# Delta rule on its two diagonal 64-token blocks: quadrant products, and the two scan directions interleaved

## The chip, the cores and the metric

One core of one Trainium2 chip runs the whole network as one program. The metric is the device time of one execution in microseconds (us); lower is better. Three runs of the kernel before took 3878.19, 3879.66 and 3897.93 us.

## The reference, cut to what matters

The reference is a stack of mixer and feed-forward blocks on 512 tokens of width 1024. Only one mixer is touched: the gated delta rule ("gdn") of the first block. It has 4 heads of key and value width 128, runs over 256 context tokens and then 512 latent tokens, once in each direction (d = 0 and d = 1), and works in chunks of 64 tokens:

```python
gc = jnp.cumsum(g, axis=-1)                                  # inside a chunk of 64
decay = jnp.exp(jnp.where(lower, gc[..., :, None] - gc[..., None, :], -jnp.inf))
lmat = jnp.where(strict, jnp.einsum('bhncd,bhnsd->bhncs', kb, k) * decay, 0.0) + jnp.eye(CHUNK)
rhs = jnp.concatenate([v * beta[..., None], kb * jnp.exp(gc)[..., None]], axis=-1)
sol = lax.linalg.triangular_solve(lmat, rhs, left_side=True, lower=True, unit_diagonal=True)
u0, kcd = sol[..., :dv], sol[..., dv:]
...
def step(s, inp):                                            # over the chunks, in order
    u = u0_i - jnp.einsum('bhcd,bhde->bhce', kcd_i, s)
    s_new = s * gl_i[..., None, None] + jnp.einsum('bhcd,bhce->bhde', kd_i, u)
    o = jnp.einsum('bhcd,bhde->bhce', qd_i, s) + jnp.einsum('bhcs,bhse->bhce', attn_i, u)
```

So each chunk needs the inverse of a unit triangular 64x64 matrix per head, some products with it, and two products per step of the recurrence.

## The kernel before, in words

Every array is fp32. The mixer treats 128 tokens (two chunks) as one **unit** (d, t): 6 tiles t of 128 tokens (t = 4, 5 are the context) in 2 directions, 12 units. The 12 units are dealt to three groups k = 0, 1, 2 of four (`gdn_front`, `self.steps`). The [128, 4, 128] tiles of a unit hold, for each of the 4 heads, a 128x128 matrix of which only the two 64x64 blocks on the diagonal are used: the two chunks. The rest is masked to zero.

A unit passes through these functions:

- `gdn_prep1` (line 881): loads a row of decays to all partitions (`gg`, line 897), forms the decay differences and their exponentials (`ga`, `gb`, on VectorE, ScalarE, GpSimd), multiplies with K K^T (TensorE, `lg<-kT`) to the matrix `gC`, and writes it to DRAM (`dC`). For latent units it also makes the masked Q K^T (`gat`) and the decayed queries (`gE`).
- `gdn_solve` (line 950), once for four units: reads the 16x16 diagonal blocks of the four `dC` back with one block per partition (`cb`), inverts them by 15 pairs of VectorE instructions (`xw`, `xb`), and writes them to `dX`.
- `gdn_prep2` (line 967): loads X (the block-diagonal inverse), transposes it to Y, and doubles the inverse twice (16 to 32 to 64) by products `lg<-gY,gC`, `lg<-gX,qz`, `lg<-qz,gX` with VectorE updates between them. Then it makes u0 and kcd (`gu`, `gkc`) by products with `gv`, and `gkd`.
- `gdn_scan` (line 1024): two steps (one for each chunk of the unit): p1 = kcd S (`sm<-gS,gkc`), uu = u0 - p1 on VectorE (`guu`), p2 = kd^T uu (`sm<-guu,gkd`), and the new state, four VectorE instructions, one for each head (`gS`). Latent units also accumulate the output (`mm<-gE,gS`, `mm<-gat,guu`), which `add_out` evicts.

`gdn_front` runs prep1 of groups 0 and 1 and both solves; at the same time the projection `ab_z` (full-size products) and the normalisation of the other mixer run. `ab_scan(k)` then runs prep2 of two units (one of each direction), their two scans, and so on; inside `ab_scan(0)` lie prep1 and the solve of group 2. The code gives a data flow: a planner orders the instructions of each engine by their priority (order in the code) and by when their inputs are ready, so groups of different units stand interleaved in each engine's queue, and each queue then runs in its order. All DMAs named here are issued from SP's queue. PSUM has banks `lg` x3, `sm` x2, `mm` x2, `lo` x1 at that time.

One fp32 product is two records in the trace, each a weight load (PEld) and a matmul (PE); the text calls such a pair a **pass**. A fp32 transpose is one.

Of the kernel before, what the change touches and what calls it, by code (L numbers as in the profile page):

```python
# [19 lines left out]
P = 128  # L20
# [11 lines left out]
class Net:  # L32
# [397 lines left out]
    def ab(self, dbg):  # L430
# [10 lines left out]
        with ExitStack() as left:  # L441
# [8 lines left out]
            lreset, masks = bp.tile([P, 256], F32, name="lreset"), bp.tile([P, 5, P], F32, name="masks")  # L450
# [343 lines left out]
    def bc4(self, ap2):  # L794

        return ap2.unsqueeze(1).to_broadcast([P, 4, P])
# [20 lines left out]
    def ab_scan(self, k, z=None):  # L817

        if k == 0:
            self.qz = []  # L820
            for l in range(2):
                for e in range(2):
                    q = self.up3.tile([P, 4, P], F32, name="qz%d%d" % (l, e))
# [45 lines left out]
    def scratch(self, zero):  # L869
        self.dC = [self.dram.tile([4, 16512], F32, name=f"dC{i}") for i in range(12)]  # L870
        self.dX = [self.dram.tile([4, 16512], F32, name=f"dX{i}") for i in range(12)]
        for t in self.dX:
            self.nc.sync.dma_start(self.whole(t), zero)

    def gtile(self, tag, bufs, pool=None):
        return (self.up2 if pool is None else pool).tile([P, 4, P], F32, name=tag, tag=tag, bufs=bufs)
# [3 lines left out]

    def gdn_prep1(self, d, t, k, i):

# [3 lines left out]
        def u(tag, bufs, pool=self.up):  # L886
            return self.gtile(tag, bufs, pool)
# [3 lines left out]
        s = slice(t * P, t * P + P)  # L891
        r0 = 32 + 32 * d
# [6 lines left out]
        self.tt(dif, self.bcl(gcc), pg, ALU.subtract)  # L899
# [4 lines left out]
        self.tt(wk[0:64], pg[0:64, :, l0], gcc[0:64], ALU.subtract)  # L904
        self.tt(wk[64:128], pg[64:128, :, l1], gcc[64:128], ALU.subtract)
# [4 lines left out]
        if lat:  # L910
            E = r["E"] = u("gE", 4, keep)
            self.act(E, pg, AF.Exp)
# [4 lines left out]
        pk = v4(self.pt("lg"))  # L917
        for h in range(4):
            self.mm(pk[:, h], kT[:, h, s], kT[:, h, s])
# [4 lines left out]
        if d == 0:  # L924
            self.tt(C, C, self.bcl(beta), ALU.mult)
        else:
            pb = u("gg", 3)
            nc.sync.dma_start(pb, self.gd[12:16, s].partition_broadcast(P))
            self.tt(C, C, pb, ALU.mult)
        nc.sync.dma_start(self.whole(self.dC[4 * k + i]), C)  # L930
        if lat:
            self.gt(r["E"], r["E"], qT[:, :, s], ALU.mult)
            pa = v4(self.pt("lg"))
            for h in range(4):
                self.mm(pa[:, h], kT[:, h, s], qT[:, h, s])
            a1 = u("gb", 2)
            self.gt(a1, Da, self.bc4(self.masks[:, 3 + d]), ALU.mult)
            at = r["at"] = u("gat", 4, keep)
            self.tt(at, a1, pa, ALU.mult)
        return r  # L940

    def whole(self, t):

        return t[:, :16384].rearrange("h (p c) -> p h c", c=P)

    def diag(self, t):

        return t.rearrange("h (b r) -> (h b) r", r=2064)[:, :2048].rearrange("b (i c) -> b i c", c=P)[:, :, 0:16]
# [18 lines left out]
    def gdn_prep2(self, d, t, k, i, r):  # L967

        nc, v4, u = self.nc, self.v4, self.gtile
# [3 lines left out]
        X = u("gX", 3, self.up3)  # L973
        nc.sync.dma_start(X, self.whole(self.dX[4 * k + i]))
        C = r.pop("C")
        pt = v4(self.pt("lg"))
        for h in range(4):
            self.tr(pt[:, h], X[:, h])
        Y = u("gY", 3, self.up3)
        nc.scalar.copy(Y, pt)  # L980
        for l in range(2):
# [3 lines left out]
            half = lambda ps: ps[:, :256].rearrange("p (h m c) -> p h m c", h=4, c=b)  # L985
            pq = half(self.pt("lg"))
            for h in range(4):
                self.mm(pq[:, h], C[:, h], part(Y, 1)[:, h])
            Q = self.qz[2 * l + self.nq % 2]
            self.tt(part(Q, 1), pq, part(self.bc4(self.masks[:, 1 + l]), 1), ALU.mult)  # L990
            if l == 0 or d == 1:
                px = half(self.pt("lg"))
                for h in range(4):
                    self.mm(px[:, h], Q[:, h], part(X, 0)[:, h])
            if l == 0 or d == 0:
                py = half(self.pt("lg"))
                for h in range(4):
                    self.mm(py[:, h], X[:, h], part(Q, 1)[:, h])
# [15 lines left out]
        for h in range(4):  # L1014
            self.mm(pu[:, h], W[:, h], vb[:, h])
        u0 = r["u0"] = u("gu0", 3)
        nc.scalar.copy(u0, pu)
        pc = v4(self.pt("lg"))
        for h in range(4):
            self.mm(pc[:, h], kb[:, h], W[:, h])  # L1020
        kc = r["kc"] = u("gkc", 3)
        nc.scalar.copy(kc, pc)

    def gdn_scan(self, d, t, r):
        nc, v4, u = self.nc, self.v4, self.gtile
        lat = t < 4
        s = slice(t * P, t * P + P)
        S = self.S[d]
        u0, kc, kd, gl = r["u0"], r["kc"], r["kd"], r["gl"]
        uu = u("guu", 2)  # L1030
        po = v4(self.pt("mm")) if lat else None
        first = True
        for j in ((0, 1) if d == 0 else (1, 0)):
            p = slice(64 * j, 64 * j + 64)
            if S is None:
                nc.vector.tensor_copy(uu[p], u0[p])
            else:
                p1 = v4(self.pt("sm"))
                for h in range(4):
                    self.mm(p1[p, h], kc[:, h, p], S[:, h])  # L1040
                self.tt(uu[p], u0[p], p1[p], ALU.subtract)
            p2 = v4(self.pt("sm"))
            for h in range(4):
                self.mm(p2[:, h], kd[p, h], uu[p, h])
            if lat:
# [917 lines left out]
```

## Time and profile before

| | |
|---|---|
| median of three runs | 3879.66 us |
| profiled execution, whole | 3887.8 us |
| its span, first to last instruction | 3885.6 us |
| TensorE busy / VectorE busy / ScalarE busy | 97% / 54% / 34% |
| stage A (prep1, solves, `ab_z`): 397 to 465 us | 68 us |
| stage B (prep2, scans): 465 to 690 us | 225 us |

The two stages are cut where the trace shows the first and the last of their instructions: the transposes of the first X start at 465 us, the last products of the last scan end near 692 us. Everything after belongs to the layers that the change doesn't touch. PE is TensorE's matmuls, PEld its weight loads, DVE is VectorE, ACT ScalarE, POOL GpSimd, SP the queue of the DMAs. PEclk is the granted TensorE clock as a share of 2.4 GHz; its two levels here are 1.0 and 0.5 (1.2 GHz). A tile written `64*128` in a row is rows x columns of the array that an instruction uses.

### The profile page before, as it was taken

Reading aid. Unit: us, or ns where it says so; the run is one execution under the profiler, and the core shown is the slowest. Engines: PE = TensorE matmul, PEld = TensorE weight load, DVE = VectorE, ACT = ScalarE, POOL = GpSimd, SP = SyncE. Lnnn points to the kernel's source line nnn. Section 1 sums busy time; section 2 is a strip of 40 time slices with the busy share of each in tenths; the row PEclk is TensorE's granted clock in tenths of the full one; section 3 lists DMA queues with packets and bytes.
Section 4 is the critical chain, followed back from the end, with each engine's and each line's share of the span. In section 5 each row is a group of like instructions: output and inputs, shape, how many; then the busy total and the mean of one; then the engine's idle time right before and its main releaser. Section 6 shows DMA issues by size and latency. Waiting matters only on the chain.

```text
span 3885.6 us, 45987 instructions
## 1 busy us (share of the span) xinstructions
PE 3763.5 (97%) x18062; PEld 3045.1 (78%) x18062; DVE 2095.3 (54%) x3391; ACT 1331.0 (34%) x2082; POOL 173.3 (4%) x200
## 2 busy tenths in 40 slices
PE   6999899999999999999999999999999999999998
PEld 3887688788878878887888748888788876788886
DVE  7656875655458863335434585434643445554345
ACT  6445511322333333224222453222432333332223
POOL 1000310000003300000000000000000000000000
PEclk9999789999999999999999999999999998999999
DMA  6411542366433233322332303333333231223332
GB/s 202 150 55 45 132 120 61 103 185 208 122 117 92 80 112 110 96 91 90 98 98 92 79 12 92 98 93 97 97 98 98 92 93 35 64 82 97 98 98 76
DMA packets 386902, 384.78 MB, mean 99 GB/s; under 512 B 40939, under 2 KB 349355, under 8 KB 386688
## 3 DMA queue, kind: packets, MB, share of 16 engines
q1 hardware_dynamic: 385720, 381.57, 32.1%
q8 instruction: 142, 2.33, 0.3%
q14 instruction: 72, 0.59, 0.0%
q10 hardware_dynamic: 968, 0.29, 0.0%
HBM read 363.47 MB, written 18.27 MB: 98 GB/s over the span
## 4 chain that ended last, share of the span: by engine, by line
PE 90%; DVE 6%; ACT 2%; issue 1%; DMA 1%; POOL 0%; DVEq 0%; SPq 0%; ACTq 0%; POOLq 0%
PE mm L145 24%; PE mm L146 24%; PE mm L147 24%; PE lg L150 3%; PE sm L150 3%; PE mm L150 3%; PE po L150 2%; PE sm L154 1%; DVE sqa L106 1%; PE po L145 1%; PE lo L150 1%; PE po L147 1%; PE po L146 1%; PE lg L145 1%; PE lg L146 0%
## 5 line engine op out<-in xcount | busy, mean ns | idle before, releaser
L106 DVE TENSOR_TENSOR wl<-wr,wh 128x1024 fp32r<-128x1024 f32 (+3 forms) x561 | 663.9, 1184 | 1126.8 <-ACT wh L120 1123.3
L145 PE MATMUL mm<-xh,wh 128*128 128x512 f32 (+1 forms) x2792 | 1093.9, 393 | 9.3 <-ACT xh L99 4.8
L146 PE MATMUL mm<-xl,wh 128*128 128x512 f32 (+1 forms) x2792 | 1092.7, 392 | 0.0
L147 PE MATMUL mm<-xh,wl 128*128 128x512 f32 (+1 forms) x2792 | 1092.0, 391 | 0.0
L120 ACT CAST wh<-wr 128x1024 fp32r<-128x1024 f32 (+3 forms) x561 | 568.2, 1014 | 1366.6 <-PE mm L146 1089.3
L145 PEld LDWEIGHTS mm<-xh,wh 128*128 128x128 f32 (+1 forms) x2792 | 525.8, 188 | 126.7 <-ACT xh L99 10.0
L147 PEld LDWEIGHTS mm<-xh,wl 128*128 128x128 f32 (+1 forms) x2792 | 525.0, 188 | 111.6 <-issue 2.1
L146 PEld LDWEIGHTS mm<-xl,wh 128*128 128x128 f32 (+1 forms) x2792 | 525.2, 188 | 110.3 <-issue 1.9
L145 PE MATMUL mm<-hh,wh 128*128 128x512 f32 x1056 | 411.3, 389 | 0.0
L147 PE MATMUL mm<-hh,wl 128*128 128x512 f32 x1056 | 410.9, 389 | 0.0
L146 PE MATMUL mm<-hl,wh 128*128 128x512 f32 x1056 | 410.8, 389 | 0.0
L145 PEld LDWEIGHTS mm<-hh,wh 128*128 128x128 f32 x1056 | 198.2, 188 | 41.2
L147 PEld LDWEIGHTS mm<-hh,wl 128*128 128x128 f32 x1056 | 198.2, 188 | 41.2
L146 PEld LDWEIGHTS mm<-hl,wh 128*128 128x128 f32 x1056 | 198.3, 188 | 41.0
L106 DVE TENSOR_TENSOR t<-mm,rstd 128x512 f32<-128x512 f32 (+1 forms) x195 | 134.3, 689 | 77.4 <-PE mm L147 73.1
L120 ACT CAST hh<-t 128x512 fp32r<-128x512 f32 x132 | 82.2, 622 | 228.9 <-DVE t L106 228.9
L117 DVE SCALAR_TENSOR_TENSOR cv<-wr,csil,cv 128x512 f32<-128x512 f32 x140 | 107.0, 764 | 46.4 <-DMA wr<-in_mod_w 44.3
L99 ACT ACTIVATE t<-t 128x512 f32<-128x512 f32 (+3 forms) x119 | 74.4, 625 | 146.5 <-DVE t L106 144.8
L1737 POOL MEMSET qk<- 2x512 f32 x32 | 16.7, 554 | 1970.8 <-PE mm L146 1797.4
L106 DVE TENSOR_TENSOR hl<-t,hh 128x512 fp32r<-128x512 f32 x132 | 90.9, 689 | 23.5 <-ACT hh L120 19.4
L117 DVE SCALAR_TENSOR_TENSOR res<-mm,res 128x512 f32<-128x512 f32 x80 | 54.9, 689 | 57.9 <-PE mm L147 57.9
L145 PE MATMUL mm<-axh,wh 128*128 128x512 f32 (+1 forms) x200 | 82.5, 413 | 1.0 <-ACT lk L682 0.8
(485 smaller groups left out, 4585.8 us busy)
## 6 DMA issues: line engine op xcount, KB each, us to landing
wr<-in_ffn_w SPq DMA_DIRECT2D x128, 512.0 KB, 3.9
wr<-in_ffa_w_gate_up SPq DMA_DIRECT2D x88, 512.0 KB, 3.5
wr<-in_ffb_w_gate_up SPq DMA_DIRECT2D x88, 512.0 KB, 3.6
wr<-in_mod_w SPq DMA_DIRECT2D x83, 512.0 KB, 3.8
wr<-in_ffa_w_down SPq DMA_DIRECT2D x40, 512.0 KB, 3.4
wr<-in_ffb_w_down SPq DMA_DIRECT2D x40, 512.0 KB, 3.5
wr<-in_ab_w_in SPq DMA_DIRECT2D x28, 512.0 KB, 3.7
wr<-in_hy_w_in SPq DMA_DIRECT2D x24, 512.0 KB, 3.7
```

What stands on the lines that cost most here:

```text
L99: return self.nc.scalar.activation(out, in_, func, **kw)
L106: return self.nc.vector.tensor_tensor(out, a, b, op=op)
L117: return self.nc.vector.scalar_tensor_tensor(out, a, s, b, op0=op0, op1=op1)
L120: self.nc.scalar.copy(hi, src)
L145: mm(ps, lhsT=wh, rhs=xh, start=first, stop=False)
L146: mm(ps, lhsT=wh, rhs=xl, start=False, stop=False)
L147: mm(ps, lhsT=wl, rhs=xh, start=False, stop=last)
L150: self.nc.tensor.matmul(ps, lhsT=lhsT, rhs=rhs, start=start, stop=stop)
L154: self.nc.tensor.transpose(ps, in_, self.ident[:k, :k])
L1737: nc.gpsimd.memset(t[64:66], 1.0)
```

## The change

- The unit's matrices hold only the two diagonal blocks: tiles of [128, 4, 64] in place of [128, 4, 128], chunk 0 on partitions 0 to 63 and chunk 1 on partitions 64 to 127. So do the masks, the `qz` buffers, `gC`, X, Y, and the DRAM scratch (`dC`, `dX`: 8 x 4160 words in place of 4 x 16512).
- Every product on them becomes two, one for each chunk, each on its own quarter of the array (rows and columns 0 to 63, or 64 to 127): K K^T, Q K^T, the transposes of X (now products with the identity), the doubling products and u0. kcd takes the row halves, into two banks.
- DMAs to and from such tiles are issued as two, one for each chunk. prep1 loads the decays a second time for the chunk-wise differences; `gat` keeps its full shape, with two GpSimd memsets for its off-diagonal blocks.
- `gdn_scan` takes both units of a pair (one of each direction). In each step the two units work on opposite chunks, and p1 and p2 are issued head by head in turn for the two units, so that neighbours lie in different halves of the array. The scaling of the old state by `gl` moves from VectorE to ScalarE (four instructions), and one VectorE addition for all heads follows.

```diff
-            for i in (i0, i0 + 1):
-                d, t = self.steps[k][i]
-                self.gdn_scan(d, t, self.st.pop((d, t)))
+            self.gdn_scan([self.steps[k][i] + (self.st.pop(self.steps[k][i]),) for i in (i0, i0 + 1)])
...
+    def cut(self, t, c):
+        return t[CH * c:CH * c + CH]
+    def rows(self, dst, i, s):
+        for c in range(2):
+            self.nc.sync.dma_start(self.cut(dst, c), self.gd[i:i + 4, s.start + CH * c:s.start + CH * c + CH].partition_broadcast(CH))
...
-        pg = u("gg", 3)
-        nc.sync.dma_start(pg, self.gd[4 * d:4 * d + 4, s].partition_broadcast(P))
+        pc = u("gg", 3)
+        self.rows(pc, 4 * d, s)
...
+        pg = u("gE", 4, keep, P) if lat else u("gF", 2, self.up, P)
+        nc.sync.dma_start(pg, self.gd[4 * d:4 * d + 4, s].partition_broadcast(P))
...
         for h in range(4):
-            self.mm(pk[:, h], kT[:, h, s], kT[:, h, s])
+            for c in range(2):
+                self.mm(self.cut(pk, c)[:, h], kT[:, h, sc[c]], kT[:, h, sc[c]])
...
-        nc.sync.dma_start(self.whole(self.dC[4 * k + i]), C)
+        self.move(self.dC[4 * k + i], C, True)
...
+        def both(ps, lhsT, rhs):
+            for h in range(4):
+                for c in range(2):
+                    self.mm(cut(ps, c)[:, h], cut(lhsT, c)[:, h], cut(rhs, c)[:, h])
...
             pq = half(self.pt("lg"))
-            for h in range(4):
-                self.mm(pq[:, h], C[:, h], part(Y, 1)[:, h])
+            both(pq, C, part(Y, 1))
...
+            p2 = [v4(self.pt("sm")) for _ in units]
             for h in range(4):
-                self.mm(p2[:, h], kd[p, h], uu[p, h])
+                for x, (d, t, r) in enumerate(units):
+                    self.mm(p2[x][:, h], r["kd"][ps[x], h], uu[x][ps[x], h])
...
-                for h in range(4):
-                    self.stt(S2[:, h], S[:, h], gl[:, h, j:j + 1], p2[:, h], ALU.mult, ALU.add)
+                    Sg = u("gSg", 2)
+                    for h in range(4):
+                        self.act(Sg[:, h], old[x][:, h], AF.Copy, scale=r["gl"][:, h, js[x]:js[x] + 1])
+                    self.tt(S2, Sg, p2[x], ALU.add)
```

## Rows read from the trace of the kernel before

**Rows 1.** The page: the span, then busy time of each engine.
```profile
span 3885.6 us, 45987 instructions
...
PE 3763.5 (97%) x18062; PEld 3045.1 (78%) x18062; DVE 2095.3 (54%) x3391; ACT 1331.0 (34%) x2082; POOL 173.3 (4%) x200
```

**Rows 2.** Busy time by stretch, A then B: stretch, length, engines, clock, DMA.
```profile
397.25:465.00 67.75, 52.59 (x277) 41.33 (x278) 59.04 (x129) 41.02 (x81) 33.92 (x31) 0.82 0.58 154
465.00:690.00 225.00, 215.63 (x1469) 189.29 (x1468) 149.62 (x340) 38.52 (x70) 23.46 (x19) 0.89 0.32 92
```

**Rows 3.** Chain of waits by line, stage A, then stage B (shares of each).
```profile
by line: DVE xw L106 14.6%; issue 13.8%; POOL gb L109 11.6%; DVE ga L106 6.5%; DVE xb L963 6.1%; DVE gC L106 5.7%; DMA gg<-gd 5.5%; DVE ndg L106 5.3%; DVE wk L106 5.2%; DVE ol L117 3.7%; DVE gat L106 2.9%; DMA dX<-xb 2.6%; DVE t L113 2.5%; 
...
by line: PE lg L150 48.3%; PE sm L150 24.3%; PE mm L150 11.9%; PE lg L154 5.1%; PE lo L150 2.3%; DVE qz L106 1.7%; issue 0.8%; ACT gY L980 0.7%; DVE gS L117 0.7%; DVE gY L106 0.6%; PE lo L147 0.5%; ACT gkc L1022 0.5%; ACT wh L120 0.4%; PE l
```

**Rows 4.** Groups of instructions, stage B, TensorE: shapes, count, busy us, mean ns, idle before.
```profile
L150 PE MATMUL lg<-gY,gC 128*128 128x64 f32 x192 | 30.0, 304 | 4.4 <-ACT gY L980 3.3 <-DVE gY L106 1.2
...
L150 PEld LDWEIGHTS sm<-guu,gkd 64*128 64x128 f32 x186 | 23.4, 191 | 3.8 <-issue 1.3 <-DVE guu L106 0.9
L150 PE MATMUL lg<-qz,gX 128*128 128x64 f32 x144 | 22.7, 308 | 1.6 <-DVE qz L106 1.6
...
L150 PE MATMUL lg<-gX,qz 128*128 128x64 f32 x144 | 21.5, 297 | 1.7 <-DVE qz L106 1.6
...
L150 PEld LDWEIGHTS sm<-gS,gkc 128*64 128x64 f32 x176 | 19.7, 145 | 6.5 <-issue 1.2 <-ACT gkc L1022 1.0 <-DVE gS L117 0.8
...
L150 PE MATMUL lg<-gv,gY 128*128 128x128 f32 x48 | 9.1, 350 | 0.2 <-DVE gY L106 0.2
```

**Rows 5.** Timeline of stage B, weight loads: start us, us, what, count.
```profile
577.90 0.97 PEld L150 LDWEIGHTS lg<-gX,qz 128*128 128x128 f32 x8 [0.17 <-issue]
...
578.79 0.97 PEld L150 LDWEIGHTS lg<-qz,gX 128*128 128x128 f32 x8
...
583.57 0.19 PEld L150 LDWEIGHTS sm<-gS,gkc 128*64 128x64 f32 x2
...
583.93 0.30 PEld L150 LDWEIGHTS mm<-gE,gS 128*128 128x128 f32 x2 [0.17 <-issue]
```

**Rows 6.** Timeline of an earlier layer part that uses quarters of the array.
```profile
212.52 0.44 PEld L150 LDWEIGHTS lg<-lvt,lkd 64*64 64x64 f32 x16 [0.36 <-ACT lkd L1118]
...
213.13 0.52 PEld L150 LDWEIGHTS lg<-gs,gla_gw 32*128 32x128 f32 x4 [0.17 <-issue]
```

**Rows 7.** Busy time by stretch at either clock level: columns as in rows 2.
```profile
489.00:499.20 10.20, 10.20 (x42) 8.78 (x41) 4.81 (x9) 0.00 (x0) 0.00 (x0) 0.50 0.29 77
...
577.70:601.60 23.90, 23.90 (x187) 21.20 (x186) 15.43 (x35) 2.25 (x4) 1.10 (x1) 1.00 0.28 72
601.60:608.40 6.80, 6.80 (x32) 5.98 (x30) 3.90 (x6) 0.58 (x1) 1.04 (x1) 0.50 0.00 0
608.40:690.00 81.60, 79.28 (x580) 67.51 (x579) 46.19 (x104) 18.42 (x31) 3.47 (x3) 1.00 0.19 60
```

**Rows 8.** Timeline of TensorE just before and in the stretch from 601.6 us.
```profile
597.81 0.83 PE L150 MATMUL lg<-gY,gC 128*128 128x64 f32 x6
598.48 1.00 PE L150 MATMUL lo<-ones,cv 128*128 128x1 f32 x8
```

**Rows 9.** Groups of instructions off TensorE: first three stage B, then two stage A.
```profile
L117 DVE SCALAR_TENSOR_TENSOR gS<-gS,gl,sm 128x128 f32<-128x128 f32 x84 | 24.6, 341 | 15.6 <-PE sm L150 15.5
...
L106 DVE TENSOR_TENSOR guu<-gu,sm 64x512 f32<-64x512 f32 x22 | 15.1, 684 | 13.8 <-PE sm L150 13.7
...
L106 DVE TENSOR_TENSOR qz<-lg,masks 128x256 f32<-128x256 f32 x24 | 10.2, 424 | 15.8 <-PE lg L150 15.7
...
L109 POOL TENSOR_TENSOR gb<-ga,masks 128x512 f32<-128x512 f32 x14 | 21.4, 1543 | 21.2 <-ACT ga L99 15.7 <-DVE ga L106 2.1 <-DVE gC L106 1.7
...
L106 DVE TENSOR_TENSOR ga<-gt,gg 128x512 f32<-128x512 f32 x10 | 11.3, 1128 | 1.4 <-DMA gg<-gd 0.7 <-ACT gb L99 0.6
```

**Rows 10.** Timeline, ScalarE on 128x128 tiles; and issue of one DMA (tile dC).
```profile
213.88 0.62 ACT L99 ACTIVATE la<-lg,gla_gb 128x128 f32<-128x128 f32 x2 [1.58 <-PE lg L150]
...
L930 SPq DMA_DIRECT2D dC<-gC x12: 359/360/367, 411.2 to 543.6; - x12
```

More of the change, by code (lines that the diff above doesn't have):

```diff
@@ L891, in gdn_prep1 @@
         s = slice(t * P, t * P + P)
+        sc = [slice(t * P + CH * c, t * P + CH * c + CH) for c in range(2)]
         r0 = 32 + 32 * d
@@ L910, in gdn_prep1 @@
         if lat:
-            E = r["E"] = u("gE", 4, keep)
+            E = r["E"] = pg
             self.act(E, pg, AF.Exp)
@@ L992, in gdn_prep2 @@
                 px = half(self.pt("lg"))
-                for h in range(4):
-                    self.mm(px[:, h], Q[:, h], part(X, 0)[:, h])
+                both(px, Q, part(X, 0))
             if l == 0 or d == 0:
                 py = half(self.pt("lg"))
-                for h in range(4):
-                    self.mm(py[:, h], X[:, h], part(Q, 1)[:, h])
+                both(py, X, part(Q, 1))
                 self.tt(part(Y, 1), part(Y, 1), py, ALU.subtract)
@@ L1024, in gdn_scan @@
-    def gdn_scan(self, d, t, r):
+        for c in range(2):
+            nc.scalar.copy(kc[:, :, CH * c:CH * c + CH], pc[c])
+    def gdn_scan(self, units):
         nc, v4, u = self.nc, self.v4, self.gtile
[L1026 to L1036, printed above, removed]
+        lat = units[0][1] < 4
+        uu = [u("guu", 2) for _ in units]
+        po = [v4(self.pt("mm")) if lat else None for _ in units]
+        first = [True, True]
+        for step in range(2):
+            js = [step if d == 0 else 1 - step for d, t, r in units]
+            ps = [slice(CH * j, CH * j + CH) for j in js]
+            old = [self.S[d] for d, t, r in units]
+            if old[0] is None:
+                for x, (d, t, r) in enumerate(units):
+                    nc.vector.tensor_copy(uu[x][ps[x]], r["u0"][ps[x]])
@@ L1037, in gdn_scan @@
             else:
[L1038 removed]
+                p1 = [v4(self.pt("sm")) for _ in units]
                 for h in range(4):
[L1040 to L1048 removed]
@@ L1049, in gdn_scan @@
-            S2 = u("gS", 3)
-            if S is None:
-                nc.vector.tensor_copy(S2, p2)
-            else:
-                for h in range(4):
-                    self.stt(S2[:, h], S[:, h], gl[:, h, j:j + 1], p2[:, h], ALU.mult, ALU.add)
-            S = S2
-        self.S[d] = S
-        if lat:
-            for h in range(4):
-                self.mm(po[:, h], uu[:, h], r["at"][:, h], False, h == 3)
-            self.add_out(0, t, po)
+                    for x, (d, t, r) in enumerate(units):
+                        self.mm(p1[x][ps[x], h], r["kc"][:, h, ps[x]], old[x][:, h])
@@ new lines, in gdn_scan @@
+                for x, (d, t, r) in enumerate(units):
+                    self.tt(uu[x][ps[x]], r["u0"][ps[x]], p1[x][ps[x]], ALU.subtract)
+            p2 = [v4(self.pt("sm")) for _ in units]
+            for h in range(4):
+                for x, (d, t, r) in enumerate(units):
+                    self.mm(p2[x][:, h], r["kd"][ps[x], h], uu[x][ps[x], h])
+            for x, (d, t, r) in enumerate(units):
+                if lat:
+                    for h in range(4):
+                        self.mm(po[x][:, h, ps[x]], old[x][:, h], r["E"][:, h, ps[x]], first[x], False)
+                        first[x] = False
+                S2 = u("gS", 4)
+                if old[x] is None:
+                    nc.vector.tensor_copy(S2, p2[x])
+                else:
+                    Sg = u("gSg", 2)
+                    for h in range(4):
+                        self.act(Sg[:, h], old[x][:, h], AF.Copy, scale=r["gl"][:, h, js[x]:js[x] + 1])
+                    self.tt(S2, Sg, p2[x], ALU.add)
+                self.S[d] = S2
@@ L1062, in add_out @@
+        if lat:
+            for x, (d, t, r) in enumerate(units):
+                for h in range(4):
+                    self.mm(po[x][:, h], uu[x][:, h], r["at"][:, h], False, h == 3)
+                self.add_out(0, t, po[x])
     def add_out(self, g, t, po):
```

83 lines of the change are left out of this document (45 added, 38 removed).

## The prediction

> **What bounds the kernel now.** I read the page first: TensorE is busy 97% of 3885.6 us [rows 1], but the delta rule fills only a small part of the span, so the share says little. I then asked the busy times of the two stretches in which its functions run. Stage A (397 to 465 us) is short of VectorE: 59.0 of 67.75 us busy, TensorE 52.6 at a mean clock of 0.82. Stage B (465 to 690 us) is short of TensorE: 215.6 of 225 us, VectorE 149.6 [rows 2]. The chain of waits agrees: in B over 90% of the pieces at its head are PE's, in A they are VectorE's and GpSimd's [rows 3]. So what TensorE saves in B counts, and what VectorE and GpSimd save counts in A.
>
> What is TensorE's time made of? Eight passes of `gX,qz` start 0.89 us before the next eight: 0.111 us each. Those move 64 columns, while the `gv` and `gC` products move 128 or 64 at the same spacing in the same queue: the load of 128 weight columns sets the step, not the columns moved [rows 4, 5]. That is the slack the change goes for. Where products of different array shapes alternate, two passes take 0.36 us (583.57 to 583.93) in place of 0.22: each change of shape costs about 0.14 us [rows 5].
>
> **TensorE in stage B, at full clock, before.** 225 us less 9.4 idle, less what the clock took: a mean of 0.89 loses 0.11 x 225 = 24.8 us [rows 2]. That leaves 191 us of work at 2.4 GHz; 1469 passes x 0.111 = 163 of it, the rest is shape changes and wide products.
>
> **The products on quarters.** The trace has such products elsewhere: 16 passes of 64*64 with 128 moving columns, loads spread over 0.44 us, and the next group, with another shape, 0.61 us after the first [rows 6]. 16 full-array passes would take 1.78 us. So quarters do run side by side; in one quarter a pass then takes about 0.11 us (four at a time in 0.44/4). The change uses only two quarters, but moves 32 columns in the doubling products. There the load is what is left: 64 columns load in less than 128 do (145 against 191 ns from end to end [rows 4]), and I take half the step, 0.055 us per quarter, two at once: 0.0275 us per pass. The other end is no better than [rows 6] per quarter: 0.055.
> - Doubling: 192 + 144 + 144 = 480 passes [rows 4] x 0.111 = 53.3 us become 960 x 0.0275 = 26.4: minus 27 (other end: 0). I take the low price, since the moving time of [rows 6] is four times that of 32 columns.
> - p1 and p2 of the scan: 176 + 186 = 362 passes [rows 4] x 0.111 = 40.2; in pairs on opposite halves they keep 128 moving columns or 128 weight columns, so 0.111 for two: 20.1, minus 20 (other end 0, if the alternation is lost).
> - K K^T and Q K^T of the four units prepared in stage B (4 x 2 x 4 heads x 2 = 64 passes, 7.1 us) become 128 on column halves, 3.5: minus 3.6.
> - u0 and kcd: four groups of 48 such as `gv,gY` [rows 4], 192 x 0.111 = 21.3, become 384 at 0.055, the same. The X transposes go from 48 passes to 192, 5.3 us either way (other end: plus 5). Both at nothing.
> - Shape changes: a group on quarters beside a full-array one costs 0.14 us at each border. Between 0 and some 168 more (seven groups in 12 units, two borders): 0 to 23 us. I take 60, plus 8, since the planner already mixes units and many borders exist.
>
> Sum: 191 - 50 + 8 = **149 us** at full clock. A page of the Trainium skill speaks against the quarters: "TensorE: Matmul & The Clock Gate", section "Wait — 56ns, not 53.3ns?", says that with the hardware decoder off the sequencer spends about 62 ns on each matmul, however short. By it the 960 passes would take 60 us and the sum would be 182. The 27 ns per pass of [rows 6] say that it doesn't hold in this run.
>
> **What lies beside TensorE in stage B.** State update: 84 instructions of 341 ns become 22 additions over 128x512 from PSUM, like `guu`'s 684 ns [rows 9]: VectorE 24.6 to 15 us, and the step from p2 to the new state falls from 4 x 0.34 to 0.68 us. The scaling goes to ScalarE, 88 x 0.31 us = 27 us [rows 10]; it needs only the old state, and ScalarE is busy 38.5 of 225 us [rows 2]: free, or 1.2 us a step if ScalarE came late. `qz`, X and Y updates halve their elements: 24 x 0.15 [rows 9] and 36 alike, minus 9 us. VectorE falls to some 125 us: not the bound. GpSimd's memsets for `gat` are hidden (23.5 of 225 us busy). The price of interleaving: both units of a pair wait at each hand-over for both `guu` (2 x 0.68 us), and p1 and p2 hold both `sm` banks. A step of a pair is about 0.9 + 0.3 + 1.4 + 0.9 + 0.3 + 1.4 = 5.2 us, twelve of them 62 us: off the path, except in the last scan. But TensorE now has less to put into the same number of hand-overs. I set its idle time at 15 us (9 as now, up to 25).
>
> **The clock.** It decides how much of this arrives. In stage B it fell to 0.50 several times although TensorE was never idle by its records: 577.7 to 601.6 us at 1.00 with 23.9 of 23.9 us busy, then 0.50 for 6.8 us, as in 489 to 499 [rows 7]. What ran just before were products of 64 moving columns and of one [rows 8], their time being weight loads. In 608.4 to 690, with the output products among them, it stayed at 1.00 [rows 7]. The change takes moving columns out and leaves loads, so I expect more low stretches: a mean of **0.80** in place of 0.89. Then stage B = 149/0.80 + 15 = 201 us: minus 24. (0.89 as now: 182, minus 43; 0.70: 228, plus 3.)
>
> **Stage A.** `ga` has 1.13 us, GpSimd's `gb` 1.54 us [rows 9]; both halve with their elements, as do `gC`, abs and exp. By unit VectorE saves some 1.5 us: 0.55 on `ga`, 0.7 on the two `gC`, 0.3 on `wk`; 8 units give 12 of its 59 us, and GpSimd about 10. Against it, SP's queue: a unit issues on average 6 DMAs in place of 2.5 (two for the chunk rows, one for the full rows, two more in half of the units, two for `gC`); 28 more x 0.36 us [rows 10] = 10 us, past which the weight loads of `ab_z` queue, and `ga` now waits for two landings. The solves' `xw`, `xb` (21% of A's chain [rows 3]) stay. I take minus 8 (0 to minus 12). X in two DMAs (12 more issues) and 24 small zero writes for 12 large ones are free: SP has room and they have long lead times; up to plus 4 if not.
>
> **Sum.** 3887.8 - 24 - 8 = 3855.8 us for the profiled execution, which lies 8.1 us above the median of the runs; on the median, 3879.7 - 32 = **3848 us**.
>
> **Rivals.**
> 1. *The clock stays low* (ends on the other side). If most of stage B runs at 1.2 GHz, TensorE needs nearly 298 us for its 149. Mean 0.60: 149/0.6 + 15 = 263, total plus 30, 3910 us; mean 0.5: 3960. It turns the sign below a mean of 0.68. For it: [rows 7, 8], and the removal of moving columns. Against it: the low stretches so far ended by themselves, since products that take double the time fill the engine, and the scan's products stay. "TensorE: Matmul & The Clock Gate", section "What's actually happening", has it that the throttle is the default and activity releases it; [rows 7] agree only in part, as a busy engine was slowed. Chance 0.17.
> 2. *Quarters don't overlap, or the alternation is lost in the queue.* The 50 us stay: 191 + 8 = 199/0.89 + 10 = 234, plus 9 - 8: 3881 us. [rows 6] are against it, but those are four quarters with long moving sides, and the planner may set other shapes between (583.57 [rows 5]). Chance 0.10.
> 3. *Hand-overs become the bound*: TensorE waits for VectorE 40 us instead of 15: 149/0.80 + 40 = 226, 3873 us. VectorE's 125 us speak against; the paired waits for it. Chance 0.14.
> 4. *The clock holds at 0.89 or better*: 182 or less, 3829 us and below. Chance 0.17.
>
> The forecast itself, mean clock about 0.72 to 0.87, has 0.42.
>
> **How the numbers follow.** Half a per cent (19 us) is about what a measurement of this kernel can tell from no change. Faster by more: rival 4 and most of the forecast, 0.56. Within: rivals 2 and 3 and the rest of it, 0.26. Slower: rival 1, 0.18. Range: the best end is 141/0.89 + 9 = 167 us and minus 12, 3810; the upper takes in rivals 2 and 3 and a mean clock down to 0.65 (244 us, 3891): 3812 to 3895.
>
> **What would show it.** Right: 16 passes of the doubling products within about 0.5 us; p1 of two units in 0.9 us; stage B near 200 us with mean PEclk near 0.8; stage A near 60. Wrong: groups of quarters at 0.1 us per pass; PEclk near 0.5 through B; PE idle before `guu` and `gS` of 30 us or more.

## The result, and the profile after

The changed kernel takes 3930.44 us (median of four runs, 3922.76 to 3945.81) against 3878.93 for the kernel before on the same chip: a ratio of 1.0127, 95% interval 1.0105 to 1.0149. It is slower by 1.3%; the prediction was 0.8% faster. Its profiled execution took 3936.05 us.

The page of the kernel after, span and busy times, for [rows 1]:

```profile
span 3934.3 us, 48067 instructions
...
PE 3787.2 (96%) x19038; PEld 3066.9 (78%) x19038; DVE 2060.1 (52%) x3321; ACT 1353.1 (34%) x2181; POOL 162.8 (4%) x216
```

Busy time by stretch, columns as in [rows 2]: stage A, stage B (here up to the last product of the last scan, 691.8 us before), and the gate after it.

```profile
397.00:467.00 70.00, 47.86 (x376) 35.70 (x375) 44.65 (x129) 35.11 (x76) 23.19 (x43) 0.80 0.46 94
467.00:723.50 256.50, 243.15 (x2340) 214.36 (x2340) 125.90 (x269) 62.93 (x171) 23.67 (x23) 0.65 0.28 78
723.50:735.30 11.80, 5.32 (x21) 2.73 (x20) 7.73 (x14) 2.86 (x7) 0.00 (x0) 0.73 0.01 1
```

VectorE is relieved in both stages as forecast (59 to 45 us, 150 to 126 us) and TensorE is still the bound of stage B, with 13 us idle. But the granted clock fell from 0.89 to 0.65. By milestones of the two traces the profiled execution lost 48.7 us: 2.2 up to the first X transpose (465.0 to 467.2), 29.3 in stage B (226.8 to 256.1), 16.2 in the **tail** from there to the first squared sum of the next layer (16.7 to 32.9), and 1 in all the rest.

TensorE's timeline in stage B, a stretch at 1.2 GHz and one at 2.4 GHz (start us, us, what, count of passes):

```profile
604.29 2.88 PE L150 MATMUL lg<-gY,gv 64*128 64x64 f32 x16
607.10 1.12 PE L150 MATMUL lg<-ident,gX 64*64 64x64 f32 x16
...
611.23 1.07 PE L150 MATMUL lg<-gX,qz 64*64 64x32 f32 x16
612.11 1.04 PE L150 MATMUL lg<-qz,gX 64*64 64x32 f32 x16
...
624.90 1.09 PE L150 MATMUL sm<-gS,gkc 128*64 128x128 f32 x8
625.91 1.10 PE L150 MATMUL mm<-gE,gS 128*128 128x64 f32 x8
...
634.72 0.66 PE L150 MATMUL lg<-gX,qz 64*64 64x32 f32 x16
635.21 0.63 PE L150 MATMUL lg<-qz,gX 64*64 64x32 f32 x16
635.77 1.77 PE L150 MATMUL mm<-gE,gS 128*128 128x64 f32 x14
...
641.35 1.74 PE L150 MATMUL lg<-gY,gv 64*128 64x64 f32 x16
643.01 0.68 PE L150 MATMUL lg<-ident,gX 64*64 64x64 f32 x16
```

Three readings. (1) A doubling group of 16 quarter passes starts the next one after 0.49 to 0.56 us at full clock (634.72, 635.21, 635.77), where 8 full-array passes took 0.89 [rows 5]: the quarters do run side by side. (K K^T and Q K^T run on column halves, 128*64, and not on quarters as the list of the change has it.) (2) Eight passes of p1 still take 1.01 us (624.90 to 625.91): the two units' products were to alternate, and don't. In the queue all four heads of one unit stand together, then four of the other; the planner has re-sorted what the code wrote in turns. (3) kcd takes 1.66 us (641.35 to 643.01) where the prediction put it at the old 0.89; it is sorted by halves in the same way.

At 1.2 GHz a group takes about 1.7 times as long, not twice: kcd 2.81 us (604.29 to 607.10) for 1.66, the doubling group 0.88 (611.23 to 612.11) for 0.49 to 0.56. So TensorE's **work at full clock** in stage B can be estimated for any run: the low share is twice what the mean clock lacks to 1, and busy time in it counts 1/1.7. After: 2 x 0.35 = 0.70 of 243.2 is 170.2, /1.7 = 100, plus 73 = 173 us. Before: 0.22 of the 217.4 us busy from 465.0 to 691.8, /1.7 = 28, plus 170 = 198. The table below uses this for all kernels (some 5 to 10 us uncertain, since the two groups give 1.6 to 1.8); tail as above. The median and the ratio are of all runs, the columns from B on of one profiled execution each.

| kernel | median us | ratio [95%] | B us | clock | work us | tail us |
|---|---|---|---|---|---|---|
| before | – | 1 | 227 | 0.89 | 198 | 17 |
| after | 3930.4 | 1.0127 [1.0105, 1.0149] | 256 | 0.65 | 173 | 33 |
| e1 padding | 3930.5 | 1.0109 [1.0062, 1.0156] | 264 | 0.62 | 173 | 27 |
| e2 wide extras | 3918.7 | 1.0092 [1.0069, 1.0114] | 219 | 0.92 | 202 | 57 |
| e3 narrow extras | 3994.9 | 1.0285 [1.0261, 1.0310] | 298 | 0.60 | 199 | 58 |
| e4 scan alone | 3898.2 | 1.0041 [1.0025, 1.0057] | 231 | 0.84 | 187 | 21 |
| e5 turns | 3910.8 | 1.0059 [1.0042, 1.0076] | 230 | 0.69 | 157 | 30 |
| e6 lean DMAs | 3912.3 | 1.0046 [1.0027, 1.0064] | 228 | 0.74 | 169 | 27 |
| e7 wide, bank lg | 3914.8 | 1.0065 [1.0045, 1.0086] | 225 | 0.90 | 204 | 28 |
| e8 quarters alone | 3932.1 | 1.0108 [1.0084, 1.0131] | 281 | 0.62 | 188 | 20 |
| e9 = e5 + e6 | 3899.0 | 1.0042 [1.0016, 1.0068] | 228 | 0.69 | 157 | 30 |
| e10 = e9 + e7 | 3914.6 | 1.0081 [1.0053, 1.0110] | 258 | 0.72 | 194 | 27 |
| e11 = e10 + first piece | 3913.0 | 1.0068 [1.0048, 1.0088] | 240 | 0.81 | 196 | 23 |
| e12 = e4 + turns | 3890.2 | 1.0014 [0.9998, 1.0030] | 230 | 0.79 | 175 | 23 |
| e13 = e11, 512 columns | 3922.5 | 1.0099 [1.0066, 1.0132] | 254 | 0.91 | 226 | 23 |
| e14 = e12 + extras | 3883.0 | 0.9987 [0.9971, 1.0004] | 221 | 0.90 | 191 | 23 |
| e15 = e9 + kcd turns, first piece | 3885.8 | 1.0005 [0.9989, 1.0021] | 224 | 0.72 | 158 | 22 |
| e16 = e15 + wide | 3890.1 | 1.0036 [1.0017, 1.0055] | 235 | 0.83 | 194 | 23 |

The kernel before, run beside each set, had medians of 3882.5 (e1 to e4), 3889.3 (e5 to e8), 3883.0 (e9 to e12), 3889.8 (e13, e14) and 3885.5 us (e15, e16). e1, e6, e9 and e16 scatter by 25 to 48 us from run to run. This scatter goes with the clock too: one program, e9, took 3876.5 us at a mean granted clock of 0.971 over the whole execution and 3924.1 at 0.958. So a profiled execution need not lie at its kernel's median (e10's is 14.5 us above it, e1's 13.5, e8's 10.1, e12's 8.9; e6's is 12.2 below, e13's 11.2, e7's 7.9), and differences of some 15 us between two rows of column B can be those of two executions and not of two kernels.

The tail. The timeline of the kernel after, where the gate ends and the output projection begins:

```profile
734.56 0.69 DVE L106 TENSOR_TENSOR xl<-om,xh 128x512 fp32r<-128x512 f32 x1 [0.68 <-ACT xh L864]
735.32 1.47 SPq L140 DMA_DIRECT2D wr<-in_ab_w_out  x3
738.79 1.04 ACT L120 CAST wh<-wr 128x1024 fp32r<-128x1024 f32 x1 [4.26 <-DMA wr<-in_ab_w_out]
739.86 1.23 DVE L106 TENSOR_TENSOR wl<-wr,wh 128x1024 fp32r<-128x1024 f32 x1 [4.61 <-ACT wh L120]
739.88 0.29 PEld L145 LDWEIGHTS lo<-xh,wh 128*128 128x128 f32 x1 [9.04 <-ACT wh L120]
```

And TensorE in the kernel before, the first and the last of the 12 output products that stood between those of the last scan:

```profile
678.19 0.80 PE L145 MATMUL lo<-xh,wh 128*128 128x512 f32 x1
...
689.23 0.40 PE L147 MATMUL lo<-xh,wl 128*128 128x512 f32 x1
```

After, the weights of the projection leave only when the gate's last `om` has been read (734.56, 735.32), and TensorE waits 9 us. In the compiled program the smaller tiles let `om` slide up by 9472 bytes, onto the buffers into which these weights are loaded; and the 12 products now stand behind the gate.

### The profile page after: what moved, and what is told of

Same layout as the page of the kernel before. It is cut to its first block, busy times and chain, and to the rows that moved or that the text cites. A ratio compares the mean times of both kernels' runs of the same rounds, so it can differ in the third digit from the quotient of the medians.

```text
span 3934.3 us, 48067 instructions
## 1 busy us (share of the span) xinstructions
PE 3787.2 (96%) x19038; PEld 3066.9 (78%) x19038; DVE 2060.1 (52%) x3321; ACT 1353.1 (34%) x2181; POOL 162.8 (4%) x216
## 4 chain that ended last, share of the span: by engine, by line
PE 89%; DVE 6%; ACT 2%; issue 1%; DMA 1%; POOL 0%; SPq 0%; DVEq 0%; ACTq 0%; POOLq 0%
PE mm L145 24%; PE mm L146 24%; PE mm L147 24%; PE lg L150 4%; PE sm L150 3%; PE mm L150 3%; PE po L150 2%; PE sm L154 1%; DVE sqa L106 1%; PE lo L150 1%; PE po L145 1%; PE po L147 1%; PE po L146 1%; ACT wh L120 0%; PE lg L145 0%
## 5 line engine op out<-in xcount | busy, mean ns | idle before, releaser
L1772 POOL MEMSET qk<- 2x512 f32 x32 | 16.7, 554 | 1969.6 <-PE mm L146 1796.6
```

Source lines behind the costliest of these rows:

```text
L1772: nc.gpsimd.memset(t[64:66], 1.0)
```

## Experiments

**e1 and e2, e3: what sets the clock.** e1 is the changed kernel with an unused tile that puts `om` back. e2 and e3 add to it, behind each doubling group, products that nobody reads, once with 256 moving columns and once two with one column each:

```diff
+            self.pad = self.up3.tile([P, 2368], F32, name="pad")          # e1, e2, e3
...
+    def extra(self, w, m):                                               # e2
+        self.mm(self.pt("lo")[:, :256], w.rearrange("p h c -> p (h c)")[:, 0:P], m.rearrange("p h c -> p (h c)"))
...
+    def extra(self, w, m):                                               # e3
+        p = self.pt("lo")
+        for i in range(2):
+            self.mm(p[:, i:i + 1], w.rearrange("p h c -> p (h c)")[:, 0:P], m.rearrange("p h c -> p (h c)")[:, i:i + 1])
```

> The changed kernel with one unused buffer of 9472 bytes per partition among the doubling's buffers, so that the buffers of the final gate (om) lie where they lay before the change, off the ring of the output projection's weights. Placement theory: the weight loads of the output projection leave by about 660 us (before 625, changed kernel 735), their products fill the last scan again, and the 16 us between the last scan product and the next layer come back: about 3914 us, with stage B unchanged at a mean clock near 0.65. Rival (the loads are late because the stage before them is late, or the tail is slow by its low clock): within 4 us of 3930.

> e1_pad, and after each of the 60 groups of doubling products one unused fp32 product on the full array with 256 moving columns: two passes, about 0.43 us at 2.4 GHz, 26 us in all. Clock theory (stage B is long because few moving columns leave the clock at 1.2 GHz): the mean clock of stage B rises from 0.65 to 0.85 or more, and although TensorE has 26 us more to do, stage B falls to about 220 us: some 36 us faster than e1_pad, near 3878. Rival (the stage is bound by the count of passes and hand-overs, the clock only goes with it): 26/0.65 = 40 us slower than e1_pad, near 3954.

> As e2_wide, but each extra is two fp32 products with one moving column (four passes, the same 0.43 us of TensorE time, nearly all weight loads). Clock theory: loads do not hold the clock, so it stays near 0.65 and the extra time comes on top: about 40 us slower than e1_pad, near 3954. Rival (any TensorE work in the gaps holds the clock, moving columns or not): as e2_wide, near 3878.

Stage B of e2, then of e3, by stretch:

```profile
466.90:685.60 218.70, 216.07 (x2427) 180.07 (x2428) 106.87 (x233) 63.00 (x171) 23.08 (x23) 0.92 0.25 63
```

```profile
469.40:767.70 298.30, 296.44 (x2548) 267.52 (x2548) 106.36 (x233) 62.22 (x171) 22.89 (x23) 0.60 0.18 46
```

The same work by the estimate (202 and 199 us), TensorE busy 99% in both, and 80 us between them: the clock is 0.92 with columns moving and 0.60 with loads in their place (e1, without extras: 0.62). One stretch of e3:

```profile
624.20:709.50 85.30, 85.30 (x577) 77.31 (x574) 19.86 (x37) 18.15 (x50) 3.11 (x3) 0.50 0.09 29
```

The clock stayed at 1.2 GHz for 85 us in which TensorE was never idle. "What's actually happening" in the Trainium skill's "TensorE: Matmul & The Clock Gate" has the throttle follow how busy the engine has been; the trace doesn't agree as far as busy time in the records goes. What differs between e2 and e3 is the kind of extra, moving columns or weight loads. Stage B came out as the clock theories had it: 219 us in e2 (220 expected), and in e3 34 us over e1 (40 expected). Neither kernel gains by it in the end: the extras sat in bank `lo`, where the modulation products `lo<-ones,cv` then waited, and the weight loads behind those (tail 57 us). e1's weight loads left at 688 in place of 735 us (660 expected), but the tail only fell to 27 us and the median not at all.

**e8 and e4: which half of the change takes the clock.** e8 has the quarters and the old scan, one unit after the other; e4 is the reverse of this diff in the kernel before: the new scan alone, with the old state update.

```diff
-            self.gdn_scan([self.steps[k][i] + (self.st.pop(self.steps[k][i]),) for i in (i0, i0 + 1)])
+            for i in (i0, i0 + 1):
+                d, t = self.steps[k][i]
+                self.gdn_scan(d, t, self.st.pop((d, t)))
```

> The changed kernel with the scan of before (one unit after the other, state update on VectorE), buffers padded as in e1_pad: quarters and chunk-wise preparation alone. Theory (the doubling on quarters takes the moving columns out, and with them the clock): mean clock of stage B 0.65 or less, stage B 255 to 265 us, 3925 to 3940. Rival (the interleaved scan is what slows the stage): stage B near 226 us at 0.8 or more, near 3890.

> The kernel before with the interleaved scan alone: both directions head by head on opposite halves, state update on VectorE as before, full-array products in the preparation as before. Clock theory: the halves do the same moving work, 20 us less TensorE time at full clock, the mean clock stays near 0.87: stage B about 211 us, 14 us less, near 3865. Rival A (waiting for both units of a pair costs more than the halves give): near 3890. Rival B (halves lower the clock too, to 0.75): stage B about 245 us, near 3900.

Stage B of e8, then of e4, by stretch:

```profile
469.30:750.20 280.90, 273.27 (x2362) 233.18 (x2363) 139.10 (x339) 38.97 (x88) 22.99 (x23) 0.62 0.30 81
```

```profile
472.00:703.40 231.40, 215.11 (x1464) 195.56 (x1462) 144.52 (x334) 37.67 (x68) 23.31 (x19) 0.84 0.29 87
```

e8 reads 281 us at 0.62, e4 231 us at 0.84 (before: 227 at 0.89). So it is the quarters that take most of the clock. e4 also shows no gain: its 187 us of work lie 11 under before, not 20; the turns are lost there too, with eight passes of one unit's p1 in a row.

**e5, e12, e15: the order.** Each product of p1 and p2 after the first is held behind the one that the code puts ahead of it (e5 on e1, e12 on e4); e15 does the same for kcd.

```diff
-                        self.mm(p1[x][ps[x], h], r["kc"][:, h, ps[x]], old[x][:, h])
+                        self.turn(self.mm(p1[x][ps[x], h], r["kc"][:, h, ps[x]], old[x][:, h]), h + x)
+    def turn(self, ins, later):
+        if later:
+            self.tc.keep_in_program_order(ins)
```

> e1_pad with the products p1 and p2 of the two units pinned to the order of the code (unit 1, unit 2, unit 1, ... by head); in the changed kernel the planner put the four heads of one unit together, so that neighbours lie in the same half of the array. Theory (the alternation was lost, which kept the scan's 20 us): a pair's p1 takes about 1.0 us where it took two times 0.95, TensorE has 20 us less to do at full clock and the same moving work in less time: 20 to 30 us less than e1_pad, 3900 to 3910. Rival (halves with 128 moving or 128 weight columns do not run side by side): within 6 us of e1_pad.

> The kernel before with the two-unit scan alone, its p1 and p2 in fixed turns; the preparation stays on the full array. e4 was this without the fixed turns: stage B 231.4 at 0.84, median 3898. If turns were all that e4 lacked: 362 passes at half the step save about 20 us at full clock, stage B about 209, median about 3876, a little under before. Rival: the paired hand-overs, not the lost turns, held e4 back; then 3890 to 3898.

> e9 (scan in fixed turns, chunk rows without extra DMAs) plus kcd's products in fixed turns of the two row halves, plus the early first piece of the output projection of e11. If the regrouping is what made kcd dear, its group of 16 passes starts the next one after about 0.9 us in place of 1.66, 9 us less work in 12 units. If the clock stays at e9's 0.69, stage B goes from 228 to about 215 us and, with a tail of 23, the median to about 3880. Rival for kcd: row halves with 64 moving columns don't overlap; 1.66 us stays. Rival for the time: the clock hands it back, stage B stays at 223 to 230, the median at about 3890.

Stage B of e1, e5 and e15 by stretch:

```profile
470.10:734.60 264.50, 251.48 (x2340) 221.85 (x2340) 126.40 (x270) 62.63 (x171) 23.91 (x23) 0.62 0.29 82
```

```profile
471.90:701.60 229.70, 211.51 (x2339) 183.91 (x2340) 126.71 (x268) 61.72 (x172) 24.49 (x23) 0.69 0.34 94
```

```profile
465.50:689.60 224.10, 205.46 (x2352) 175.04 (x2353) 134.42 (x298) 61.70 (x172) 24.52 (x24) 0.72 0.31 88
```

TensorE's timeline in e5, then in e15:

```profile
626.57 1.09 PE L150 MATMUL sm<-gS,gkc 128*64 128x128 f32 x14
627.59 1.10 PE L150 MATMUL mm<-gE,gS 128*128 128x64 f32 x8
...
630.26 1.16 PE L150 MATMUL sm<-guu,gkd 64*128 64x128 f32 x14
631.35 1.60 PE L150 MATMUL mm<-gat,guu 128*128 128x128 f32 x12
```

```profile
626.33 1.11 PE L150 MATMUL lg<-gY,gv 64*128 64x64 f32 x16
627.37 0.68 PE L150 MATMUL lg<-ident,gX 64*64 64x64 f32 x16
```

Fourteen of the 16 passes of a pair's p1 now take 1.02 us, where after took 1.01 for the eight of one unit; p2 1.09; kcd 1.04 for 16 in place of 1.66. All three alternate as soon as the queue keeps the order. In e12 the work falls from 198 to 175 us, near the 20 us of the prediction. But stage B takes 230 us as in e4, since the clock went from 0.84 to 0.79; and e15's 158 us of work at 0.72 take 224. The work arrived, and in these two profiled executions the clock took nearly all of it.

It isn't always so. From e1 to e5 the clock rose from 0.62 to 0.69, stage B fell by 35 us, and the median, 3911, is at the upper end of the 3900 to 3910 expected. By the ratios of all runs, fixed turns are worth 0.5% (e5 against e1) and 0.3% (e12 against e4), some 20 and 10 us, both at the edge of the intervals. e12's median is at its rival's 3890; e15's lies between theory (3880) and rival (3890), its stage B where the rival has it.

**e6: SP's queue.** The chunk-wise differences, `wk` and the scaling of C come out of the full rows in two VectorE instructions of 64 partitions, without the extra DMAs.

```diff
-        pc = u("gg", 3)
-        self.rows(pc, 4 * d, s)
+        own = lambda a, c: self.cut(a, c)[:, :, CH * c:CH * c + CH]
-        self.tt(dif, self.bcl(gcc, CH), pc, ALU.subtract)
+        for c in range(2):
+            self.tt(self.cut(dif, c), self.bcl(self.cut(gcc, c), CH), own(pg, c), ALU.subtract)
```

> e1_pad without the second load of the decays: prep1 takes the chunk-wise differences from the full rows, in two VectorE instructions of 64 partitions, and the beta rows come in one DMA; 3.5 DMAs per unit in place of 6. Queue theory (SP's queue, 43.5 us of issue time in stage A against 21 before, holds stage A and pushes the weight loads of the modulation columns back, and these the output projection's): the first of these weight loads leaves near 470 us (before 450, changed kernel 495), stage A is some 4 us shorter, the tail after the last scan product falls from 27 towards 17 us: about 3916. Rival (SP's queue has room, the loads are late by the length of stage B): VectorE's 0.9 us more per unit, 3930 to 3936.

Issue times (ns, min/median/max): the halves in after, the whole rows (128 partitions) in after, and one whole DMA of e6 that replaces two halves:

```profile
L886 SPq DMA_DIRECT2D gg<-gd x36: 573/615/1602, 401.3 to 507.1; - x36
...
L961 SPq DMA_DIRECT2D dC<-gC x24: 574/602/1472, 410.2 to 544.0; - x24
```

```profile
L912 SPq DMA_DIRECT2D gE<-gd x8: 367/603/605, 428.7 to 484.1; - x8
```

```profile
L942 SPq DMA_DIRECT2D gF<-gd x6: 359/468/1272, 408.1 to 448.7; - x6
```

A DMA on 64 partitions took SP 0.57 us or more (median 0.60 to 0.62), one on 128 partitions 0.36 before [rows 10]. The number of partitions isn't all of it: the whole rows of after, right behind halves in the queue, took 0.60 too, and one that stood alone 0.37. So two halves cost 1.2 us where one whole costs 0.36 to 0.60. With e6's edit SP's issues in stage A fell from 43.5 to 32.8 us (before: 21.1).

Stage A itself starts 401 to 408 us into the execution, differently from kernel to kernel, so its length is better read from the first load of decays to the first X transpose. It is 64 to 65 us in the four kernels with the old preparation (before, e4, e12, e14), 65 to 68 in the seven with the change's DMAs, and 56 to 59 in the seven with e6's edit (e6, e9, e10, e11, e13, e15, e16). The edit is worth some 7 us there. Part of that may be stage A's clock (0.88 to 0.90 with the edit, 0.80 in after).

The loads of the modulation columns left at 443 us in e6 (after: 495), but the tail stayed at 27 us, so the queue theory's way to 3916 isn't what happened. That the median, 3912, came near it is luck: stage B of e6 took 228 us at 0.74 where e1's took 264 at 0.62, though the edit hardly touches stage B's work (169 against 173 us). Why the clock differs there stays open; the two executions also lie on opposite sides of their medians. The Trainium skill's "DMA: Bandwidth & Descriptors", "Rules for kernel authors", advises against two transfers to disjoint partition halves. It does so because both use the same engines, which no run here tests; the issue times point the same way.

**e7, e9, e10, e13, e14, e16: putting it together.** e7 is e2 with the extras in bank `lg`; e9 to e16 are the sums named in the table; e13's extras move 512 columns; e14 adds to e12 one full-array product of 128 columns behind each doubling group.

```diff
-        self.mm(self.pt("lo")[:, :256], w.rearrange("p h c -> p (h c)")[:, 0:P], m.rearrange("p h c -> p (h c)"))  # e2
+        self.mm(self.pt("lg")[:, :256], w.rearrange("p h c -> p (h c)")[:, 0:P], m.rearrange("p h c -> p (h c)"))  # e7, e10, e11, e16
...
+        self.mm(self.pt("lg"), w.rearrange("p h c -> p (h c)")[:, 0:P], self.tab["kT"][:, 0, 0:T])  # e13
...
+            self.mm(self.pt("lg")[:, :P], C[:, 0], C[:, 0])               # e14, and so for Q and X
```

> e2_wide with the unused products written to the bank group lg in place of lo, which the modulation columns need: in e2_wide these columns came only at the end and the tail took 57 us. Clock theory: stage B near 219 us at a mean clock of 0.9 as in e2_wide, and the tail near 27 us as in e1_pad: about 3889. Rival (the extras delay the columns through TensorE's queue wherever they write): tail again above 45 us, 3910 to 3920.

> The alternation of p1 and p2 by a fixed order (as in e5) and the chunk rows without the extra DMAs (as in e6), together, with the padding that puts om back. If the two gains are independent: e6 had stage B 228.5 us and a median of 3912, e5 took 20 us off stage B at the same padding, so stage B is about 207 and the median about 3893. Rival: with 20 us less work the array moves fewer columns in the same time and the granted clock of stage B falls from 0.74 to 0.66 or less; then stage B is 220 or more and the median 3905.

> e9 plus the wide products on bank lg behind each doubling group (as in e7; they write a bank that nobody reads and only keep columns moving). Clock theory: stage B at a clock near 0.90 in place of e9's 0.70, so the 24 us that the extra products cost are more than paid back: stage B about 203, first X at 462, tail still 27 to 28, median about 3876, level with before. Rival: with the alternation kept the clock is high enough without the extras, and they only cost: stage B 215 to 225, median at or above e9's.

> e11 with extra products of 512 moving columns in place of 256 behind each doubling group, 60 of them, about 25 us more work at full clock than e11. If e11 and e10 lacked moving columns, the clock of stage B rises from 0.82 (e11) and 0.72 (e10) to 0.93 or more, and stage B takes about 220 us although it has more to do; median about 3893. Rival: it is the fixed order of the scan's products that lowers the clock; then it stays near 0.80, stage B is 265 us or more, median about 3938.

> e12 with one more full-array product of 128 moving columns behind each doubling group on the full array (60 of them, some 13 us at full clock; nobody reads them). e12 had 168 us of work at full clock, 18 us of idle time and a clock of 0.79. If moving columns hold the clock at 0.90, stage B is 181/0.9 + 18 = 219 us in place of 230, median about 3879, level with before. Rival: 128 columns are too few to matter; then the clock stays at 0.79, stage B is 247 us, median about 3907.

> e15 plus the wide extra products of 256 columns of e7, e10 and e11. Those three had the clock at 0.90, 0.72 and 0.82. At 0.90 the 187 us of work at full clock take about 212 us, median about 3877; at 0.75, 240 us and 3905. It pays against e15 only if the clock comes out above 0.85.

Stage B of e12 and of e14 by stretch:

```profile
469.00:699.30 230.30, 211.81 (x1474) 191.13 (x1473) 148.28 (x338) 38.52 (x69) 23.68 (x19) 0.79 0.31 94
```

```profile
468.20:688.90 220.70, 208.31 (x1593) 187.17 (x1592) 148.63 (x338) 38.31 (x69) 23.28 (x19) 0.90 0.33 98
```

e14 came out as the clock theory had it: 16 us more work, 10 us less time. e7 also did in stage B (225 us at 0.90), but its median, 3915, is 26 us over the 3889 expected. In stage B e9's rival won: 157 us of work took the same 228 us as e6's 169, the clock fell from 0.74 to 0.69; the median, 3899, lies between the two. **e10 missed**: the extras of e7, and yet 0.72. e13, with twice the columns and the same fixed order, is back at 0.91, so the order as such doesn't hold the clock down; but its extras cost 30 us of work where 25 were reckoned, and stage B took 254, not 220. e16 read 0.83, between the two cases, and didn't pay. Why the same extras gave 0.90, 0.72, 0.81 and 0.83 in e7, e10, e11 and e16 stays open. They differ in what stands between the extras, but part of it can be the execution: e10's profiled one was the slowest of its four (3929 us, the others 3910 to 3919), and the medians of e7, e10 and e11 lie within 2 us of each other.

**e11: the tail.** The first piece of the output projection is loaded and cast ahead of the last scans, and its 24 products are placed ahead of the projection's loop.

```diff
+            w0 = self.raw(self.w3(A["ab_w_out"][0], 0, 256, 4, 4), 4, 256)
+            self.split(wh0, wl0, w0)
             self.ab_scan(2, z)
```

> e10 plus the first piece of the output projection loaded and cast ahead of the last scans, so that 12 of its products on bank lo stand in TensorE's queue before the last gate, as they did in the kernel before. If the missing 12 products are what lengthens the tail: the tail goes from 27 or 28 to 20 to 23 us, and the median is 5 to 8 us below e10's, about 3870. Rival: the tail is the two gates that now end side by side, and stays at 27.

The tail fell from 26.8 (e10) to 22.9 us; its twelve products on `lo` ran from 633.8 us on. The median fell by 1.7 us only, within the scatter. With e1 this divides the 16 us: some 6 from `om`'s place (32.9 to 27.2), 4 from the 12 products, and 3 more lie between the last scan product and the end of the last gate (8.4 us before, 11.3 after, 14.3 in e12). That both units of the last pair now end at once doesn't explain these 3: in e8 they end one after the other as before, and it is 11.3 us there too. They and the other 3 to 4 us stay open; the granted clock of the tail was 1.00 before and 0.74 in after, which may be part of it.

## Why the prediction was wrong

- **The clock: the step that failed.** By the prediction's own way, busy time times clock, after has 243.2 x 0.65 = 158 us of work, against 149 forecast, and 13 us idle, against 15. At the forecast's 0.80 that would be 158/0.80 + 13 = 211 us, 10 over the 201; at 0.65 it is 256. So the clock is 45 of the 55 us by which stage B was missed. (By the table's estimate it is 36: 173 us of work would take 220 us at 0.80.) It was rival 1, with a chance of 0.17 (mean 0.60: 263 us, total 3910). The reason held against it, that low stretches end by themselves because slow products fill the engine, didn't hold: e3 stayed at 1.2 GHz for 85 us with the engine busy throughout. What was right is the reading of [rows 7, 8], that columns and not occupancy go with the clock; it was given too little weight. The value of 0.80 came from no row.
- **The clock is not all.** With 0.65 in place of 0.80 the prediction's own sum gives 244 us for stage B and 3891 in all, still inside its range. The other 39 us are 12 of work in stage B, 10 in stage A, 16 in the tail and 1 in the rest. The chances also took the rivals as excluding each other, while rival 1 and the second half of rival 2 (the lost alternation, part of a chance of 0.10) came together.
- **Quarters** (doubling minus 27 us): right in kind, 0.49 to 0.56 us a group in place of 0.44. The 8 us for changes of shape were not measured by themselves.
- **p1 and p2** (minus 20): none of it in after. "In turns" was a property of the code, not of the queue. The prediction named this in rival 2 and as its other end; e5 and e12 show both the loss and the price.
- **u0 and kcd at nothing**: kcd costs 0.8 us a unit more, 9 us in 12 units at full clock, by the same re-sorting (e15).
- **VectorE and hand-overs**: right. VectorE 126 us (125 forecast), idle 13. The groups below are what the new update costs: the sum at 686 ns as forecast, the scaling at 391 ns where 310 was taken, without consequence.

```profile
L106 DVE TENSOR_TENSOR gS<-gSg,sm 128x512 f32<-128x512 f32 x22 | 15.1, 686 | 12.5 <-PE sm L150 12.4
```

```profile
L99 ACT ACTIVATE gSg<-gS,gl 128x128 f32<-128x128 f32 x88 | 28.5, 391 | 41.9 <-DVE gS L106 35.7 <-DVE gS L1084 3.2 <-DVE oc L855 2.7
```

- **Stage A** (minus 8): plus 2. VectorE's saving came (14 us), but the term for SP's issues was mis-sized: 0.36 us was the price of a DMA on 128 partitions that stands alone; the halves, and the wholes behind them, took 0.60. With e6's edit stage A came out 5 to 8 us shorter than before, near the forecast.
- **The tail** wasn't in the sum at all: 16 us. Smaller tiles moved other tiles (6 us, e1), and 12 products that had stood among the last scan's came behind the gate (4 us, e11); the rest is open.

So of some 80 us between the forecast for the profiled execution (3855.8) and its time, some 53 are stage B (mostly the clock), 10 stage A and 16 the tail. No version was measurably faster than the kernel before; e12 (1.0014), e14 (0.9987) and e15 (1.0005) are level with it. The table shows how little the work alone says: in eight of its kernels, before among them, from 204 us of work (e7) down to 157 (e5, e9), stage B takes 224 to 231 us, while the clock runs from 0.90 down to 0.69; in the other ten it takes 219 to 298 us.

## What to carry to other kernels

Before saving TensorE time by packing small products, look at the granted clock of that stage: where it already drops, products with fewer moving columns may give the time back through the clock, so price the change at the lower level too. If a gain rests on neighbours in the queue, read the order in the program that was built, or pin it. Keep a transfer in one DMA over all partitions, and look at where tiles move when their neighbours shrink. Where executions of one kernel differ by 20 us, don't read a stage's gain from one trace of each.

## What the runs showed of the hardware

- With TensorE 99% busy the granted clock can stay at 1.2 GHz for most of a 298 us stage (0.60), 85 us of it at a stretch (e3); one extra product of 256 columns behind each doubling group in place of two of one column lifted it to 0.92 (e2), at the same work by the estimate.
- The same program can be granted different clocks: e9's ten executions run from 3876.5 us at 0.971 to 3924.1 at 0.958.
- Saved work need not be saved time there: e12 and e15 have some 20 and 40 us less of it than the kernel before, yet stage B took 230 and 224 us against 227 in the profiled executions, and the whole is level with before (1.0014 and 1.0005).
- Products on opposite halves of the array overlapped as direct neighbours, 14 passes of p1 in 1.02 us (e5), and hardly when sorted by unit, 8 in 1.01 (after).
- At half the clock, two groups of short passes took about 1.7 times as long, not twice (after).
- Issuing a DMA that touches 64 partitions took 0.57 us or more; one on 128 partitions took 0.36 alone and 0.60 right behind a half (before and after).
